# A mixture-of-experts layer on one core: the first token page gathered ahead of the sorting, the arrangement in the second pass, recurrence constants behind the modulation, the overflow branch behind the stores

## The chip, the cores and the metric

One core of a Trainium2 chip runs one hand-written kernel. The metric is the device time of the whole program in microseconds (us), the median over several runs; a profile is one further execution with the hardware profiler. The engines are TensorE (PE; its weight loads are shown apart as PEld), VectorE (DVE), ScalarE (ACT), GpSimd (POOL) and SyncE (SP, which issues nearly all DMA transfers here). Each engine works through its own queue in order and waits for others by semaphores.

## The reference

A layer with 256 latent tokens and 256 context tokens of width 1024: modulation, an input projection, a bidirectional recurrence (RG-LRU) beside a pooling group, an output projection, and then a top-4-of-32 mixture of experts, which has nearly all the weights. All is in float32. Cut to what matters:

```
mod_l = silu(c) @ w_mod + b_mod
h     = layer_norm(x + pos) * (1 + sc1) + sh1
z     = h @ w_in                                # 1536 columns
log_a = -8 * r * softplus(-lam)                 # recurrence constants
x1    = layer_norm(alpha * x + g1 * (mix @ w_out))
t     = x1 * (1 + sc2) + sh2                    # 256 tokens
logits = t @ router_w + router_b
top_v, top_i = top_k(logits, 4);  top_p = softmax(top_v)
for e in range(32):                             # only the chosen tokens count
    gu  = t @ w1[e] + b1[e]                     # w1[e]: 1024 x 2048
    act = clamped_swiglu(gu)
    out += gate[:, e] * (act @ w2[e] + b2[e])   # w2[e]: 1024 x 1024
y = layer_norm(alpha * x1 + g2 * out) * ln2_g + ln2_b
```

## The kernel before, in words

**Weights.** All weights come through a list made ahead of time, `plan` (L66 on): modulation weights, input projection, output projection, then for each expert position p the eight blocks of `w1` and the four blocks of `w2` of position p - 1. A block is 1024 KB. `due()` (L133) hands the next entries of the list to whichever slot of SBUF has come free, in the order in which slots come free, and `load()` issues them on SP. There are 12 ring slots, and eight more that earlier stages give up. The first two expert positions are always experts 0 and 1, so their weights need no index; from position 2 on, `source()` (L103) reads the expert's number from `ord_i` into a register of SP (L106).

**Prefix.** x and ctx are normalised and turned (`norm0`, `turn0`); the modulation vectors come from `gemv` and `mod_cols` (L370 to L380), and DVE and ACT apply shift and scale block by block (L437). In the program text the recurrence constants `hgb`, `aln` and the softplus of `lru_lambda` (L394 to L417, some 28 small DVE operations and an Exp on ACT) stand between the first modulation vector and the second. PE then makes the projections z (`z_block`, L444), followed by convolution, gates, scan, pooling, output projection, and the second norm.

**Routing.** `route`, `top4a`, `top4b` choose four experts for each token. `place(h)` (L677) counts, for each token and expert, how many earlier tokens chose it: `posm`, the token's place in the expert's list. For h = 1 it calls `sort` (L699): DVE compares the counts and makes the permutation S, two small matmuls (L710, L711) bring expert numbers and counts into that order, `ord_i` and `exc_i` are copied out. `softmax` (L791) makes the gates.

**Expert loop.** Chosen tokens are put into groups of 32 slots; expert position p has `SEQ[p]` groups (56 in all), and four groups make a page. For a page, `maps` (L816) builds a 0/1 matrix Pm from `slot` and a column of posm, `gather` (L836, two halves of 16 matmul passes, into the PSUM tile "misc") multiplies by it to bring the tokens into slots, and ACT copies the result to `xe`. `column` takes the first two positions' columns from posm and gate themselves, later ones from `placed`, which is in sorted order. `gated` (L826) makes Pg, Pm times the gates, and `turn_map` (L849) turns it, for `combine` (L926), which adds the results to the token accumulators acc[t][h].

A pass serves one or two groups of one expert: `gemm1` (L855) with eight k-steps, bias, `swiglu`, then `second` (L1036), which runs `gemm2` (L904) of the pass before. `gemm1` takes `hooks`: at k-step i it calls hooks[i], so other PE work is put between its steps: `turn` (turns the activations of the pass before, hook 1), `turn_map` (hook 3), `gather` of the next page (hooks 4 and 6). All these use the one PSUM tile "misc", emptied by ACT or DVE. `retire` gives slots of an expert's last pass back, one block at each k-step.

`arrange` (L942) stands before the first pass: posm and gate are turned (L948), brought into sorted order by S (L960, giving `placed`), and the experts' output biases, as Y, are added to acc with the gates (L968).

**Order.** The section from the expert loop on has a fixed order of instructions on each engine, the order of the program text.

**End.** Behind the last pass's `turn` comes `overflow()` (L977): all engines read the largest excess over a group's capacity into a register, and where it is positive they run a body that handles the surplus tokens. Then `second` of the last pass, `combine`, the last norm (`moments`, `scales`, `finish`) and the stores.

Of the kernel before, what the change touches and what calls it, by code (L numbers as in the profile page):

```python
# [56 lines left out]
def hybrid(tc, a, out):  # L57
# [175 lines left out]


# [4 lines left out]
    with ExitStack() as px:  # L239
# [171 lines left out]
        for n in (13, 11, 9, 7, 5, 3, 1):  # L411
# [5 lines left out]
        dve.tensor_scalar(hs, l0, -4.0, None, op0=ALU.mult)  # L417

        pool.iota(slot, pattern=[[1, P]], base=1, channel_multiplier=0, allow_small_or_imprecise_dtypes=True)
        tri = sb.tile([P, P], BF16, name="tri")  # L420
        one1 = sb.tile([P, 1], BF16, name="one1")
        ones = one1.to_broadcast([P, P])
        pool.memset(one1, 1.0)
        pool.memset(tri, 1.0)
        pool.affine_select(
            out=tri, in_=tri, pattern=[[1, P]], compare_op=ALU.is_gt, fill=0.0, base=0, channel_multiplier=-1
        )

        pool.tensor_scalar(x, x, ALPHA, None, op0=ALU.mult)
        sc1 = mod_cols(1, C_BM + 8, 1.0)  # L430
        for j in range(KD):
            for i in range(2):
                seg = hT(j)[:, T * i : T * i + T]
                if j % 2:
                    act.activation(seg, seg, AF.Identity, bias=sh1[:, i, j : j + 1], scale=sc1[:, i, j : j + 1])
                else:
                    dve.tensor_scalar(seg, seg, sc1[:, i, j : j + 1], sh1[:, i, j : j + 1], op0=ALU.mult, op1=ALU.add)  # L437

# [238 lines left out]
        def place(h):  # L677
# [18 lines left out]
            if h:  # L696
                sort(pp[:, 1, :], pp[:, 2, 0:1])

        def sort(cnt, cntc):  # L699

            key = sb.tile([P, NE], F32, name="key")
            keyc = sb.tile([P, 2], F32, name="keyc")
            dve.scalar_tensor_tensor(key, cnt, 64.0, col(C_KR, NE), op0=ALU.mult, op1=ALU.add)
            dve.scalar_tensor_tensor(keyc[:, 0:1], cntc, 64.0, col(C_KC), op0=ALU.mult, op1=ALU.add)
            dve.tensor_copy(keyc[:, 1:2], cntc)
            dve.tensor_scalar(key, key, keyc[:, 0:1], None, op0=ALU.is_gt)
            dve.tensor_reduce(keyc[:, 0:1], key, axis=AX.X, op=ALU.add)
            dve.tensor_scalar(S, col(C_RK, NE), keyc[:, 0:1], None, op0=ALU.is_equal)
            sp2 = mm.tile([1, 2, NE], F32, tag="mm", name="sp2")
            pe.matmul(sp2[:, 0, :], col(C_EI)[0:NE], S[0:NE], start=True, stop=True)  # L710
            pe.matmul(sp2[:, 1, :], keyc[0:NE, 1:2], S[0:NE], start=True, stop=True)  # L711
            for c in range(4):
                dve.tensor_scalar(SM[:, c, :], S, col(C_MASK + c), None, op0=ALU.mult)
            dve.tensor_copy(ord_i, sp2[:, 0, :])
            exc = key[0:1]
            dve.tensor_tensor(exc, sp2[:, 1, :], cols[0:1, C_CAP : C_CAP + NE], op=ALU.subtract)
            dve.tensor_scalar(exc, exc, 0.0, None, op0=ALU.max)
            dve.max(cmx, exc)
            dve.tensor_copy(exc_i[:, 0:NE], exc)
            dve.tensor_copy(exc_i[:, NE : NE + 1], cmx[:, 0:1])  # L720

# [29 lines left out]
        place(0)  # L751
        residual(1)
        top4a(1, lp)
        top4b(1)
        bp = mm.tile([P, T], F32, tag="mm", name="bp")
        for c in range(4):
            pe.matmul(
                bp[32 * c : 32 * c + 32, :],
                ident[:, 32 * c : 32 * c + 1].to_broadcast([P, 32]),
                bgrow[:, 1, :],  # L760
                start=True,
                stop=True,
                skip_group_check=True,
            )
        place(1)
        act.activation(g2s, bp, AF.Copy)
        donate("aa")
# [22 lines left out]

    def softmax(h):  # L791
        lh, nh = lg[:, h, :], ng[:, h : h + 1]
        dve.tensor_scalar(lh, lh, mx[:, h, 0:1], None, op0=ALU.subtract)
        act.activation(lh, lh, AF.Exp)
        dve.tensor_tensor(lh, lh, ge[:, h, :], op=ALU.mult)
        dve.tensor_reduce(nh, lh, axis=AX.X, op=ALU.add)
        dve.reciprocal(nh, nh)
        dve.tensor_scalar(gate[:, h, :], lh, nh, None, op0=ALU.mult)

# [35 lines left out]

    def gather(Pm, xe, k4):  # L836

        gx = misc([P, 4, P])
# [102 lines left out]

    def arrange():  # L942

        gt = misc([P, 4, P])
        for m, src in enumerate((posm, gate)):
            for h in range(2):
                for c in range(4):
# [7 lines left out]
                    )  # L955
        GT = spare[:, 0:4]
        act.activation(GT, gt, AF.Copy)
        so = misc([P, 4, NE])
        for m in range(4):
            pe.matmul(so[:, m], GT[0:NE, m], S[0:NE], start=True, stop=True)  # L960
        dve.tensor_copy(placed, so)
        for c in range(4):
            dve.scalar_tensor_tensor(
                Y[:, T * c : T * c + T], b2, col(C_MASK + c), g2s, op0=ALU.mult, op1=ALU.mult
            )
        for h in range(2):
            for t in range(2):
# [9 lines left out]
    def overflow():  # L977

        n_max = nc.values_load(exc_i[0:1, NE : NE + 1], engines=engines, min_val=0, max_val=T)
        with tc.If(n_max > 0, preferred_fallthrough_block=False):  # L980
# [11 lines left out]
            with tc.For_i(0, NE, 1) as i:  # L992
                n_i = nc.values_load(exc_i[0:1, bass.ds(i, 1)], engines=engines, min_val=0, max_val=T)
                with tc.If(n_i > 0):
# [15 lines left out]
                    for j in range(2):  # L1010
                        with tc.If(n_i > P * j):
# [41 lines left out]
    for n, (p, gs) in enumerate(passes):  # L1053
# [37 lines left out]
    turn(done[0], aT)  # L1091
    overflow()
    second(*done[1:], aT)
    back = (Y, PgT)

# [32 lines left out]

    for t in range(2):
        for h in range(2):  # L1130
            combine(*back, t, h, 0, 256)
            combine(*back, t, h, 256, 512)
            dve.bn_stats(st[:, t, h, :], acc[t][h])  # L1133
            if (t, h) == (1, 0):
                scales(0)
                finish_pool(0, 1)
        moments(t)
    finish(0, 0)
    store(0, 0)
    store(0, 1)  # L1140
    scales(1)
    finish_pool(1, 1, 256)
    finish(1, 0)
    store(1, 0)
    finish(1, 1, 0, 256)
    store(1, 1)
    order.close()
# [94 lines left out]
```

## Time and profile before

| | us |
|---|---|
| median of 3 runs | 1142.4 |
| the three runs | 1142.13, 1142.4, 1144.59 |
| the profiled execution's own time | 1143.31 |
| its span in the profile | 1141.6 |
| PE busy | 987.2 (86%) |
| DVE busy | 304.3 (27%) |
| ACT busy | 164.4 (14%) |
| POOL busy | 54.9 (5%) |
| bytes moved | 444.78 MB, 390 GB/s in the mean |

The span runs from the first to the last instruction of the profiled execution; its own time has 1.7 us more around it. A matmul that reads float32 is shown as two records. Of the 444.78 MB nearly all are weights, in blocks of 1024 KB. The granted clock of PE over the span is 0.945 of full speed.

### The profile page before, as it was taken

Reading aid. Unit: us, or ns where it says so; the run is one execution under the profiler, and the core shown is the slowest. Engines: PE = TensorE matmul, PEld = TensorE weight load, DVE = VectorE, ACT = ScalarE, POOL = GpSimd, SP = SyncE. Lnnn points to the kernel's source line nnn. Section 1 sums busy time; section 2 is a strip of 40 time slices with the busy share of each in tenths; the row PEclk is TensorE's granted clock in tenths of the full one; section 3 lists DMA queues with packets and bytes.
Section 4 is the critical chain, followed back from the end, with each engine's and each line's share of the span. In section 5 each row is a group of like instructions: output and inputs, shape, how many; then the busy total and the mean of one; then the engine's idle time right before and its main releaser. Section 6 shows DMA issues by size and latency. Waiting matters only on the chain. (4 is left out here: it accounts for less than half of the span.)

```text
span 1141.6 us, 21794 instructions
## 1 busy us (share of the span) xinstructions
PE 987.2 (86%) x9237; PEld 422.3 (37%) x9238; DVE 304.3 (27%) x803; ACT 164.4 (14%) x347; POOL 54.9 (5%) x73
## 2 busy tenths in 40 slices
PE   7799987999999968969997797869989887999663
PEld 3356554344334412424433232324433233443222
DVE  5436461132123121121321211212131221313104
ACT  3245331101110100101000110000100110110001
POOL 2128200000000000000000000000000000000001
PEclk9899998999999988979999999989999898999896
DMA  9999683999999999999999999999999999999992
GB/s 355 350 379 368 265 351 115 417 416 416 416 417 417 417 418 417 415 417 415 416 417 416 416 416 416 417 417 416 417 416 417 417 416 417 417 414 407 416 405 100
DMA packets 89862, 444.78 MB, mean 390 GB/s; under 512 B 9304, under 2 KB 15576, under 8 KB 56992
## 3 DMA queue, kind: packets, MB, share of 16 engines
q1 hardware_dynamic: 89528, 443.01, 96.0%
q8 instruction: 75, 1.23, 0.4%
q10 hardware_dynamic: 232, 0.32, 0.1%
q14 instruction: 27, 0.22, 0.1%
HBM read 442.25 MB, written 1.05 MB: 388 GB/s over the span
## 5 line engine op out<-in xcount | busy, mean ns | idle before, releaser
L862 PE MATMUL ph<-blk,xe 128*32 128x512 f32 x3584 | 427.8, 608 | 48.9 <-DMA blk<-in_w_dram 48.1
L911 PE MATMUL py<-blk,aT 128*32 128x256 f32 x3584 | 226.0, 405 | 67.1 <-DMA blk<-in_w_dram 60.5
L862 PEld LDWEIGHTS ph<-blk,xe 128*32 128x32 f32 x3584 | 103.7, 111 | 292.2 <-issue 170.5
L911 PEld LDWEIGHTS py<-blk,aT 128*32 128x32 f32 x3584 | 118.2, 116 | 185.5 <-issue 71.9
L924 DVE TENSOR_TENSOR Y<-py,g2s 32x256 f32<-32x256 f32 x224 | 94.2, 420 | 245.1 <-PE py L911 242.3
L889 DVE TENSOR_SCALAR av<-ph 128x256 f32<-128x256 f32 x56 | 23.6, 422 | 481.0 <-PE ph L876 481.0
L902 ACT ACTIVATE aT<-misc 128x256 f32<-128x256 f32 (+1 forms) x38 | 18.4, 485 | 395.1 <-PE misc L901 386.6
L845 ACT ACTIVATE xe<-misc,AB 128x128 f32<-128x128 f32 x112 | 42.1, 456 | 172.3 <-PE misc L842 172.3
L842 PEld LDWEIGHTS misc<-Pm,blk 128*128 128x128 f32 x448 | 54.0, 197 | 27.3 <-issue 22.6
L842 PE MATMUL misc<-Pm,blk 128*128 128x128 f32 x448 | 59.4, 288 | 4.3 <-DVE Pm L821 2.5
L444 PE MATMUL zp<-blk 128*128 128x256 f32 (+1 forms) x192 | 59.8, 468 | 3.7 <-DVE blk L437 3.7
L876 PE MATMUL ph<-b,SM 128*32 128x512 f32 x448 | 57.5, 616 | 0.0
L890 ACT ACTIVATE sgm<-av 128x256 f32<-128x256 f32 x56 | 23.3, 416 | 217.6 <-DVE av L889 217.6
L928 PE MATMUL acc<-Y,PgT 128*128 128x512 f32 (+1 forms) x120 | 51.9, 576 | 0.5 <-DVE Y L924 0.5
L1122 POOL TENSOR_TENSOR blk<-blk 128x512 f32<-128x512 f32 (+1 forms) x2 | 2.0, 992 | 977.0 <-ACT blk L1121 977.0
L444 PEld LDWEIGHTS zp<-blk 128*128 128x128 f32 x192 | 37.3, 196 | 25.7 <-issue 21.6
L928 PEld LDWEIGHTS acc<-Y,PgT 128*128 128x128 f32 x120 | 21.4, 189 | 31.2 <-issue 21.4
L876 PEld LDWEIGHTS ph<-b,SM 128*32 128x32 f32 x448 | 15.0, 114 | 35.6 <-issue 35.6
L590 PE MATMUL acc<-blk 128*128 128x512 f32 x64 | 27.8, 592 | 0.0
L892 DVE SCALAR_TENSOR_TENSOR av<-l,av 128x256 f32<-128x256 f32 x56 | 23.8, 425 | 10.9 <-ACT sgm L890 9.4
L359 PE MATMUL gp<-blk,csil 128*32 128x256 f32 x384 | 22.6, 382 | 2.4 <-DMA blk<-in_w_mod_dram 2.4
L893 DVE TENSOR_TENSOR av<-av,sgm 128x256 f32<-128x256 f32 x56 | 23.8, 425 | 1.9
(211 smaller groups left out, 451.3 us busy)
## 6 DMA issues: line engine op xcount, KB each, us to landing
blk<-in_w_dram SPq DMA_DIRECT2D x383, 1024.0 KB, 20.0
blk<-in_w_mod_dram SPq DMA_DIRECT2D x23, 1024.0 KB, 10.6
blk<-in_w_in_dram SPq DMA_DIRECT2D x6, 1024.0 KB, 16.9
blk<-in_w_out_dram SPq DMA_DIRECT2D x4, 1024.0 KB, 5.2
blk<-in_ctx_dram SPq DMA_DIRECT2D x2, 512.0 KB
blk<-in_x_dram SPq DMA_DIRECT2D x2, 512.0 KB
blk<-in_w_mod_dram SPq DMA_DIRECT2D x2, 512.0 KB, 16.4
blk<-in_w_dram SPq DMA_DIRECT2D x2, 512.0 KB
```

The source lines that it names most:

```text
L444: pe.matmul(zp[:, :n], w[:, k, P * half : P * half + P], hT(k)[:, :n], start=(k == 0), stop=(k == KD - 1))
L590: pe.matmul(acc[h][half], mixT[:, k, P * h : P * h + P], weight("out", k // 2)[:, k % 2, 512 * half : 512 * half + 512], start=(k == 4), s ...
L842: pe.matmul(gx[:, kk], xn[:, t, P * k : P * k + P], Pm[:, t], start=(t == 0), stop=(t == 1))
L845: act.activation(xe[:, k], gx[:, kk], AF.Identity, bias=AB[:, 1, k : k + 1], scale=AB[:, 0, k : k + 1])
L862: pe.matmul(ph[32 * c : 32 * c + 32], x[:, k], wv[:, :, c, :], start=(k == 0), stop=False, skip_group_check=True,)
L876: pe.matmul(ph[32 * c : 32 * c + 32], sel[c].to_broadcast([P, GS]), b1, start=False, stop=True, skip_group_check=True,)
L889: dve.tensor_scalar(av, ph[:, 0, :], 7.0, None, op0=ALU.min)
L892: dve.scalar_tensor_tensor(av, l1, 8.0, av, op0=ALU.min, op1=ALU.mult)
L893: dve.tensor_tensor(av, av, sgm, op=ALU.mult)
L911: pe.matmul(py[32 * c : 32 * c + 32, i], aT[:, i, k % 2, k // 2, :], W[k // 2][:, k % 2, T * c : T * c + T], start=(k == 0 and i == 0), st ...
L924: dve.tensor_tensor(dst[:, T * c : T * c + T], py[r, i], g2s[r], op=ALU.mult)
L928: pe.matmul(acc[t][h][:, lo:hi], PgT[:, P * t : P * t + P], Y[:, 512 * h + lo : 512 * h + hi], start=False, stop=False, skip_group_check=True,
```

## The change

Four things are done. The names are those above.

1. **First page ahead of the sorting.** `sort` is split. `place(1)` only makes `key` and `keyc`, which are now persistent tiles; then the maps of page 0 are built, and the comparisons of `sort_a` and the gates (`softmax_b`) follow. On PE the first gather half stands ahead of `sort_b`'s two matmuls, which use a "ph" tile; the second half goes into the tile "py". The subtraction and Exp of the softmax (`softmax_a`) move into the prefix.
2. **Arrangement in the second pass.** `arrange` is split into three. In pass 1, hook 0 is `arrange_a` (turning posm and gate), hook 1 `turn`, hook 2 `arrange_b` (sorted order, `placed`, the maps of page 1, the biases Y), hook 3 `turn_map`, hooks 4 and 6 the two gather halves of page 1, and `arrange_c` (biases to acc) stands before `second`. Pass 0 has no hooks. GT has a tile of its own. In later pages with two passes the second gather half moves from hook 4 to hook 5.
3. **Constants later.** The recurrence constants stand behind the loop that applies the modulation.
4. **Branch behind the stores.** `overflow`'s branch stands after the last norm and the stores; its register loads stand ahead of the last position's gemm1, and its body ends with a second `last_norm()` without the combine.

```
-            if h:
-                sort(pp[:, 1, :], pp[:, 2, 0:1])
+                dve.scalar_tensor_tensor(key, pp[:, 1, :], 64.0, col(C_KR, NE), op0=ALU.mult, op1=ALU.add)
+                dve.scalar_tensor_tensor(keyc[:, 0:1], pp[:, 2, 0:1], 64.0, col(C_KC), op0=ALU.mult, op1=ALU.add)
+                dve.tensor_copy(keyc[:, 1:2], pp[:, 2, 0:1])
...
+    def sort_a():
+        dve.tensor_scalar(key, key, keyc[:, 0:1], None, op0=ALU.is_gt)
+        dve.tensor_reduce(keyc[:, 0:1], key, axis=AX.X, op=ALU.add)
+        dve.tensor_scalar(S, col(C_RK, NE), keyc[:, 0:1], None, op0=ALU.is_equal)
...
+    def sort_b(sp2):
+        pe.matmul(sp2[:, 0, :], col(C_EI)[0:NE], S[0:NE], start=True, stop=True)
+        pe.matmul(sp2[:, 1, :], keyc[0:NE, 1:2], S[0:NE], start=True, stop=True)
+        dve.tensor_copy(ord_i, sp2[:, 0, :])
...
-    softmax(0)
-    softmax(1)
-    spare = wk.tile([P, KD, P], F32, name="xe")
+    GT = wk.tile([P, 4, P], F32, name="GT", bufs=1)
     ahead = page_maps(0)
-    for k4 in range(2):
-        gather(*ahead, k4)
+    sort_a()
+    for h in range(2):
+        softmax_b(h)
+    gather(*ahead, 0)
+    sort_b(ps.tile([1, 2, NE], F32, tag="ph", name="sp2", bufs=2))
     Pg = gated(0, ahead[0])
+    gather(*ahead, 1, "py")
     act.activation(wk.tile([P, 1], F32, name="sgm0", bufs=1), zero, AF.Sigmoid)
-    arrange()
...
-            hooks[3] = lambda PgT=PgT, Pg=Pg: turn_map(PgT, Pg)
-            if more:
+            if n:
+                hooks[3] = lambda PgT=PgT, Pg=Pg: turn_map(PgT, Pg)
+            if more and n:
                 ahead = page_maps(page + 1)
-        if more and len(of_page[page]) == 2:
-            hooks[4 if at else 6] = lambda at=at: gather(*ahead, at)
+        if n == 1:
+            hooks = {0: arrange_a, 2: arrange_b, 3: lambda: turn_map(PgT, Pg)}
+            hooks.update({4 + 2 * j: lambda j=j: gather(*ahead, j) for j in range(2)})
+        elif n and more and len(of_page[page]) == 2:
+            hooks[5 if at else 6] = lambda at=at: gather(*ahead, at)
...
+        if p == NE - 1:
+            n_max = nc.values_load(exc_i[0:1, NE : NE + 1], engines=engines, min_val=0, max_val=T)
...
+        if n == 1:
+            arrange_c()
         if done:
             second(*done[1:], aT)
...
     turn(done[0], aT)
-    overflow()
     second(*done[1:], aT)
...
+    last_norm((Y, PgT))
+    overflow()
```

PE from the last routing matmul (pp, L687 before and L701 after) to the first expert's gemm1 (ph); sp is the tile of the two sort matmuls, Pm the page map, Y the biases, blk weights or tokens. Before:

```order
L687 MATMUL pp<-one_337,selb 32x1
L710 MATMUL sp_1112<-S,cols 1x32
L711 MATMUL sp_1112<-S,keyc 1x32
L842 MATMUL misc<-Pm,blk 128x128 x16
L948 MATMUL misc<-ident,posm 32x128 x8
L948 MATMUL misc<-ident,gate 32x128 x8
L960 MATMUL misc<-S,xe 128x32 x4
L968 MATMUL acc<-Y,xe 128x512 x4
L862 MATMUL ph<-blk,xe 32x512 x32
```

After:

```order
L701 MATMUL pp<-one_306,selb 32x1
L847 MATMUL misc<-Pm,blk 128x128 x8
L793 MATMUL sp_1161<-S,cols 1x32
L794 MATMUL sp_1161<-S,keyc 1x32
L847 MATMUL py<-Pm,blk 128x128 x8
L867 MATMUL ph<-blk,xe 32x512 x64
L881 MATMUL ph<-b_72,SM 32x512 x8
```

The two sort matmuls now stand between the gather halves, the second of which writes to py; the matmuls of the arrangement have left this place. The first pass's gemm1 is in one piece.

PE in the second pass, from its first k-steps to the gemm2 (py from blk and aT); av are activations being turned, Pg the gated map. Before, from the last hooked work of the first pass on:

```order
L862 MATMUL ph<-blk,xe 32x512 x24
L842 MATMUL misc<-Pm,blk 128x128 x8
L862 MATMUL ph<-blk,xe 32x512 x8
L876 MATMUL ph<-b_72,SM 32x512 x8
L862 MATMUL ph<-blk,xe 32x512 x16
L901 MATMUL misc<-ident,av_1344 128x128 x2
L901 MATMUL misc<-ident,av_1345 128x128 x2
L862 MATMUL ph<-blk,xe 32x512 x24
L842 MATMUL misc<-Pm,blk 128x128 x8
L862 MATMUL ph<-blk,xe 32x512 x24
L876 MATMUL ph<-b_72,SM 32x512 x8
L911 MATMUL py<-blk,aT 32x256 x64
```

After:

```order
L953 MATMUL misc<-ident,posm 32x128 x8
L953 MATMUL misc<-ident,gate 32x128 x8
L867 MATMUL ph<-blk,xe 32x512 x8
L906 MATMUL misc<-ident,av_1287 128x128 x2
L906 MATMUL misc<-ident,av_1288 128x128 x2
L867 MATMUL ph<-blk,xe 32x512 x8
L967 MATMUL misc<-S,GT 128x32 x4
L867 MATMUL ph<-blk,xe 32x512 x8
L857 MATMUL misc<-ident,Pg 128x128 x2
L867 MATMUL ph<-blk,xe 32x512 x8
L847 MATMUL misc<-Pm,blk 128x128 x8
L867 MATMUL ph<-blk,xe 32x512 x16
```

The first two parts of the arrangement (posm, gate; S) now stand between gemm1's k-steps; the second gather half follows two k-steps later, and the third part (`acc<-Y,GT`) stands behind the bias and ahead of gemm2.

DVE in the prefix, from the last copy of the turned ctx (tr) to the modulation of the blocks (mc is the modulation's column, blk the tokens). Before, the end of that stretch (hgb and aln, L395 and L396, stand directly behind the copies):

```order
L412 TENSOR_TENSOR hs<-hs,l_307 128x8
L413 TENSOR_SCALAR hs<-hs 128x8
L414 SCALAR_TENSOR_TENSOR l_306<-l_306,hs 128x8
L415 TENSOR_SCALAR l_305<-l_305 128x8
L416 TENSOR_TENSOR l_305<-l_305,l_306 128x8
L417 TENSOR_SCALAR hs<-l_305 128x8
L380 SCALAR_TENSOR_TENSOR mc<-cp,cols 128x8 x2
L437 TENSOR_SCALAR blk<-blk,mc 128x256 x8
```

After:

```order
L337 COPY blk<-tr 128x2x256 x2
L394 SCALAR_TENSOR_TENSOR mc<-cp,cols 128x8 x2
L425 TENSOR_SCALAR blk<-blk,mc 128x256 x8
L429 TENSOR_SCALAR hgb<-cols 128x16
L430 TENSOR_SCALAR aln<-cols 128x16
L437 TENSOR_SCALAR l_375<-cols 128x8
L438 TENSOR_TENSOR l_376<-l_375,cols 128x8
```

The column mc and the modulation stand directly behind the copies, ahead of hgb and aln.

## Rows read from the trace of the kernel before

**Rows 1.** The page, achieved DMA rate in the 40 slices of 28.5 us.

```profile
GB/s 355 350 379 368 265 351 115 417 416 416 416 417 417 417 418 417 415 417 415 416 417 416 416 416 416 417 417 416 417 416 417 417 416 417 417 414 407 416 405 100
```

**Rows 2.** Stretches: bounds, length, busy us (instructions) per engine, clock, DMA share, GB/s.

```profile
172.00:175.20 3.20, 2.51 (x13) 2.54 (x14) 1.35 (x9) 0.00 (x0) 0.00 (x0) 0.67 1.03 407
175.20:195.40 20.20, 14.80 (x102) 8.21 (x104) 2.78 (x11) 4.98 (x11) 0.00 (x0) 0.80 0.04 8
...
200.00:1100.00 900.00, 793.79 (x8076) 313.36 (x8068) 196.66 (x550) 87.37 (x213) 0.00 (x0) 0.95 1.02 416
```

**Rows 3.** Timeline of PE, 168.6 to 192 us: start, length, instruction [idle before].

```profile
172.69 3.38 PE L842 MATMUL misc<-Pm,blk 128*128 128x128 f32 x16 [2.55 <-DVE Pm L821]
177.78 2.05 PE L842 MATMUL misc<-Pm,blk 128*128 128x128 f32 x16 [1.72 <-ACT xe L845]
181.43 0.65 PE L948 MATMUL misc<-ident,posm 128*32 128x128 f32 x16 [1.59 <-ACT xe L845]
...
183.43 1.91 PE L960 MATMUL misc<-S,xe 32*128 32x32 f32 x8 [0.92 <-ACT xe L957]
186.51 5.50 PE L968 MATMUL acc<-Y,xe 128*128 128x512 f32 x8 [1.17 <-DVE Y L963]
191.94 0.64 PE L862 MATMUL ph<-blk,xe 128*32 128x512 f32 x4
```

**Rows 4.** Timeline of DVE, the same stretch.

```profile
168.91 0.15 DVE L705 COPY keyc<-pp 128x1 f32<-128x1 f32 x1
...
171.97 0.74 DVE L821 TENSOR_SCALAR Pm<-slot,posm 128x64 f32<-128x64 f32 x4
```

**Rows 5.** Timeline of PE, 210 to 420 us.

```profile
229.49 7.09 PE L911 MATMUL py<-blk,aT 128*32 128x256 f32 x128
...
244.47 7.07 PE L862 MATMUL ph<-blk,xe 128*32 128x512 f32 x64
...
270.66 3.70 PE L928 MATMUL acc<-Y,PgT 128*128 128x512 f32 x8
```

**Rows 6.** Timeline of DVE, 26 to 38 us.

```profile
26.26 5.35 DVE L396 TENSOR_SCALAR aln<-cols 128x16 f32<-128x16 f32 x1
...
36.54 0.23 DVE L380 SCALAR_TENSOR_TENSOR mc<-cp,cols 128x8 f32<-128x8 f32 x2
```

**Rows 7.** Timeline of PE, 26 to 46 us.

```profile
33.24 0.61 PE L377 MATMUL cp<-ident,part 128*128 128x8 f32 x4 [0.50 <-ACT part L373]
37.57 8.70 PE L444 MATMUL zp<-blk 128*128 128x512 f32 x13 [3.72 <-DVE blk L437]
```

**Rows 8.** Timeline of all engines, 14 to 75 us.

```profile
16.12 10.85 SPq L156 DMA_DIRECT2D blk<-in_w_in_dram  x2
...
26.20 5.38 POOL L429 TENSOR_SCALAR blk<-blk 128x2048 f32<-128x2048 f32 x1 [20.14 <-PE tr L317]
```

**Rows 9.** The page's DMA issues: count, KB each, median us to landing.

```profile
blk<-in_w_in_dram SPq DMA_DIRECT2D x6, 1024.0 KB, 16.9
```

**Rows 10.** Stretches, columns as in rows 2.

```profile
36.00:44.00 8.00, 6.43 (x9) 2.74 (x10) 3.34 (x14) 4.04 (x8) 0.00 (x0) 0.57 1.11 282
```

**Rows 11.** Timeline of PE, 1104 us to the end.

```profile
1113.91 0.69 PE L901 MATMUL misc<-ident,av 128*128 128x128 f32 x2
1121.19 5.92 PE L911 MATMUL py<-blk,aT 128*32 128x256 f32 x64 [6.59 <-issue]
```

**Rows 12.** The line of the branch: count, ns min/median/max, first and last start.

```profile
L980 SPq COMPARE_BRANCH  x2: 38/48/57, 1107.8 to 1123.6; - x2
L980 PEldq COMPARE_BRANCH  x2: 95/3091/6087, 1112.8 to 1114.9; - x2
```

**Rows 13.** Waits of SP: us in total, times, longest.

```profile
SPq L980 <- SPq L980: 15.1, 1, 15.1
```

**Rows 14.** Stretches, columns as in rows 2, behind SP's jump.

```profile
1123.20:1126.20 3.00, 3.00 (x37) 1.61 (x33) 0.00 (x0) 0.00 (x0) 0.00 (x0) 0.63 0.03 8
```

More of the change, by code (lines that the diff above doesn't have):

```diff
@@ L204, in hybrid @@
     cmx = const.tile([1, 8], F32, name="cmx")
+    key = const.tile([P, NE], F32, name="key")
+    keyc = const.tile([P, 2], F32, name="keyc")
     lnrow = const.tile([P, 2, T], F32, name="lnrow")
@@ L232, in spread, with softmax_a, softmax_b @@
             act.activation(dst[:, 512 * c2 : 512 * c2 + 512], bp.rearrange("p c n -> p (c n)"), AF.Copy)
+    def softmax_a(h):
+        lh = lg[:, h, :]
+        dve.tensor_scalar(lh, lh, mx[:, h, 0:1], None, op0=ALU.subtract)
+        act.activation(lh, lh, AF.Exp)
+    def softmax_b(h):
+        lh, nh = lg[:, h, :], ng[:, h : h + 1]
+        dve.tensor_tensor(lh, lh, ge[:, h, :], op=ALU.mult)
+        dve.tensor_reduce(nh, lh, axis=AX.X, op=ALU.add)
+        dve.reciprocal(nh, nh)
+        dve.tensor_scalar(gate[:, h, :], lh, nh, None, op0=ALU.mult)
     accp = es.enter_context(tc.tile_pool(name="acc", bufs=1, space=PSUM))
@@ L391, in hybrid @@
         turn0(0)
+        pool.iota(slot, pattern=[[1, P]], base=1, channel_multiplier=0, allow_small_or_imprecise_dtypes=True)
+        tri = sb.tile([P, P], BF16, name="tri")
+        one1 = sb.tile([P, 1], BF16, name="one1")
+        ones = one1.to_broadcast([P, P])
+        pool.memset(one1, 1.0)
+        pool.memset(tri, 1.0)
+        pool.affine_select(
+            out=tri, in_=tri, pattern=[[1, P]], compare_op=ALU.is_gt, fill=0.0, base=0, channel_multiplier=-1
+        )
+        pool.tensor_scalar(x, x, ALPHA, None, op0=ALU.mult)
+        sc1 = mod_cols(1, C_BM + 8, 1.0)
+        for j in range(KD):
+            for i in range(2):
+                seg = hT(j)[:, T * i : T * i + T]
+                if j % 2:
+                    act.activation(seg, seg, AF.Identity, bias=sh1[:, i, j : j + 1], scale=sc1[:, i, j : j + 1])
+                else:
+                    dve.tensor_scalar(seg, seg, sc1[:, i, j : j + 1], sh1[:, i, j : j + 1], op0=ALU.mult, op1=ALU.add)
         hgb = sb.tile([P, 16], F32, name="hgb")
@@ L417, in hybrid @@
         dve.tensor_scalar(hs, l0, -4.0, None, op0=ALU.mult)
[L419 to L437, printed above, removed]
         def z_block(blk, half, n):
@@ L696, in place @@
             if h:
-                sort(pp[:, 1, :], pp[:, 2, 0:1])
[L699 to L720, printed above, removed]
+                dve.scalar_tensor_tensor(key, pp[:, 1, :], 64.0, col(C_KR, NE), op0=ALU.mult, op1=ALU.add)
+                dve.scalar_tensor_tensor(keyc[:, 0:1], pp[:, 2, 0:1], 64.0, col(C_KC), op0=ALU.mult, op1=ALU.add)
+                dve.tensor_copy(keyc[:, 1:2], pp[:, 2, 0:1])
         def residual(h):
@@ L752, in hybrid @@
         residual(1)
+        softmax_a(0)
         top4a(1, lp)
@@ L764, in hybrid @@
             )
+        act.activation(g2s, bp, AF.Copy)
+        softmax_a(1)
         place(1)
-        act.activation(g2s, bp, AF.Copy)
         donate("aa")
@@ L789, in misc @@
         return ps.tile(shape, F32, tag="misc", name="misc")
[L791 to L798, printed above, removed]
+    def sort_a():
[6 more added lines that the diff above has]
+        dve.tensor_copy(ord_i, sp2[:, 0, :])
+        exc = key[0:1]
+        dve.tensor_tensor(exc, sp2[:, 1, :], cols[0:1, C_CAP : C_CAP + NE], op=ALU.subtract)
+        dve.tensor_scalar(exc, exc, 0.0, None, op0=ALU.max)
+        dve.max(cmx, exc)
+        dve.tensor_copy(exc_i[:, 0:NE], exc)
+        dve.tensor_copy(exc_i[:, NE : NE + 1], cmx[:, 0:1])
+        for c in range(4):
+            dve.tensor_scalar(SM[:, c, :], S, col(C_MASK + c), None, op0=ALU.mult)
     def column(m, h, p):
@@ L834, in gated, with gather @@
         return Pg
-    def gather(Pm, xe, k4):
-        gx = misc([P, 4, P])
+    def gather(Pm, xe, k4, tag="misc"):
+        gx = ps.tile([P, 4, P], F32, tag=tag, name=tag)
         for kk in range(4):
@@ L940, in combine_all, with arrange_a @@
                 combine(Y, PgT, t, h)
-    def arrange():
+    def arrange_a():
         gt = misc([P, 4, P])
@@ L955, in arrange, with arrange_b @@
                     )
-        GT = spare[:, 0:4]
         act.activation(GT, gt, AF.Copy)
+    def arrange_b():
+        nonlocal ahead
         so = misc([P, 4, NE])
@@ L961, in arrange @@
         dve.tensor_copy(placed, so)
+        ahead = page_maps(1)
         for c in range(4):
@@ L965, in arrange, with arrange_c @@
             )
+    def arrange_c():
         for h in range(2):
@@ L1026, in overflow @@
                 dve.tensor_scalar(num, num, 1.0, None, op0=ALU.add)
+            last_norm()
     def page_maps(page):
@@ L1127, in store, with last_norm @@
         sp.dma_start(ov[:, t, s], y2[:, t, s])
[L1129 to L1146, printed above, removed]
+    def last_norm(back=None):
+        for t in range(2):
+            for h in range(2):
+                if back:
+                    combine(*back, t, h, 0, 256)
+                    combine(*back, t, h, 256, 512)
+                dve.bn_stats(st[:, t, h, :], acc[t][h])
+                if (t, h) == (1, 0):
+                    scales(0)
+                    finish_pool(0, 1)
+            moments(t)
+        finish(0, 0)
+        store(0, 0)
+        store(0, 1)
+        scales(1)
+        finish_pool(1, 1, 256)
+        finish(1, 0)
+        store(1, 0)
+        finish(1, 1, 0, 256)
+        store(1, 1)
+    last_norm((Y, PgT))
+    overflow()
     order.close()
```

2 lines of the change are left out of this document (removed).

## The prediction, made before the changed kernel ran

> **What bounds the kernel now.** I read the 40 slices first. From slice 8 to the last but one the weights arrive at 405 to 418 GB/s; in slice 7 the rate falls to 115 [rows 1]. So the long expert loop runs at the pace of the weight stream, and the reader is to see in it only that a stream started earlier ends earlier by as much. The finer windows show the hole: 407 GB/s up to 175.2, 8 GB/s from 175.2 to 195.4, and 416 in the loop behind it [rows 2]; some 20 us of streaming are missing. The timeline says why. All 20 weight slots are full, and the first comes free when the first expert's GEMM has used a block; that GEMM starts at 191.94 [rows 3], although the last selection result is there at 168.91 + 0.15 = 169.1 [rows 4]. Between lie softmax, sort, page map, two gather halves and the arrangement, one after the other. Two smaller places: the start of the projections [rows 6, 7] and the end, where TensorE (PE) stands from its transpose at 1113.91 to 1121.19 [rows 11].
>
> **Gather ahead of sort, arrangement in the second pass.** VectorE (DVE) now builds the page map right behind the counts: four operations, 0.74 us [rows 4], ready at 169.8. PE's first gather half follows. Its row of before took 3.38 us behind an idle gap, the second half 2.05 [rows 3]; with only about a microsecond of idle left I take 2.05 (range 2.05 to 3.38). The two sort matmuls, 32 columns each, are smaller than the first arrangement group of 0.65 us [rows 3]; I take 0.3 for the pair. The second half goes into a PSUM bank of its own, so it no longer waits for ScalarE (ACT) to empty the first, as its row of before does: 2.05 more. Sum 169.8 + 2.05 + 0.3 + 2.05 = 174.2, and the GEMM starts there instead of at 191.94: **17.7 us** earlier (15.1 with both halves at 3.38). ACT fills the first four blocks of the gathered page during the second half, and the GEMM asks for them one by one. The softmax sums, masks and gates that DVE still does afterwards lie beside the first pass's GEMM, two groups of 7.07 [rows 5]. The order of experts is copied out about 2 us later than before; SyncE (SP) waits for it with all later expert loads behind it, but the first of those needs a freed slot at about 176, so this wait is covered.
>
> The arrangement comes back inside the second pass. Its first part runs from 181.43 to the end of its matmuls at 182.5, 1.1 us of PE; the second took 1.91 and the third 5.50 [rows 3], both in a stretch of lowered clock. For the second I take half, 0.95; for the third, eight passes of 128x512, the combine's row of the same shape and count, 3.70 [rows 5]. Together 5.8 us more between the start of the first GEMM and that of the first second-layer GEMM, which before was 229.49 - 191.94 = 37.6 [rows 3, 5] and becomes 43.4.
>
> Does the stream feel that? The first block is freed a quarter of 7.07 us, 1.8, after the GEMM starts, and the stream was back at 195.4 [rows 2], 3.5 after the start, so 1.7 go from freeing to flowing. A block of 1024 KB [rows 9], 1.049 MB, takes 2.5 us at 416 GB/s. The 16 first-layer blocks of experts 0 and 1 feed it for 40.3 us, to start + 43.8. The 17th slot is a second-layer block, free at start + 43.4 + 1.8 and flowing 1.7 later, at 46.9: a new hole of about **3.1 us**. Before, the same sum gave 37.6 + 3.5 = 41.1, ahead of 43.8. Net at the front 17.7 - 3.1 = 14.6.
>
> **Constants later.** DVE's queue holds the softplus chain ahead of the modulation. Its second operation stretches to 5.35 us beside the 5.38 us in which GpSimd (POOL) scales x [rows 6, 8], and the chain ends just before 36.54, where the modulation's scale is made [rows 6]; the product it waits for was done at 33.24 + 0.61 = 33.85, and PE starts 1.03 us after the scale, at 37.57 [rows 6, 7]. Behind the change the scale follows at 33.9 and PE at 34.9. The weights for it were issued at 16.12 [rows 8] and such blocks take 16.9 us in the median [rows 9], 33.0, so they hardly hold it up: **2.6 us**. The chain then runs beside the first projections; its consumer, the first gate exponential, comes three projections later. There is a second gain: behind PE's idle stretch the granted clock is 0.57 on average from 36 to 44, with PE busy 6.43 us of it [rows 10], so 6.43 x 0.43 = 2.8 us are lost to the clock there. With the gap down to 1 us this may be won or not: I take 2.0 of 0 to 2.8. From there to the selection PE is nearly always busy, so its start moves everything: 4.6 us.
>
> **Branch behind the stores.** Before, PE reaches the branch, and its jump alone takes 6087 ns from 1114.9 [rows 12], to 1121.0. Without it PE could start the last GEMM at about 1115.1. But SP waits at that branch for 15.1 us [rows 13] before its jump, last seen at 1123.6 [rows 12]; I read this wait as that for the last weights, landed at 1123.0, since the stream too has ended by then [rows 14]. The last of eight GEMM steps needs them, 5.92/8 = 0.7 us [rows 11]. The GEMM ends at 1123.8 instead of 1121.19 + 5.92 = 1127.1: 3.3 gained, not 6. At the end every engine now jumps after its last work. PE's 6.1 us lie beside normalisation and stores. SP ends last; its steps there cost 1123.6 - 1123.0 = 0.6. Its jump is bounded by its own 57 ns and by PE's 6.1 [rows 12]; 8 GB/s x 3 us = 24 KB were moved in the 3 us behind SP's jump, with no weight or store under way [rows 14], so I take half of that stretch, 1.5. Net 3.3 - 0.6 - 1.5 = **1.2 us**. The counts' register loads, now ahead of the last expert's GEMM, fall where PE waits for weights, and on SP behind the last weight issue: nothing.
>
> On that jump the Trainium skill (Runtime: NRT & Kernel Launch, Instruction fetch mechanics) says that a taken branch whose target lies outside the fetched window waits for a fetch; PE's row agrees, and by it the stall would not go away but move to whichever engine ends the program. That is the third rival below.
>
> **Sum.** 14.6 + 4.6 + 1.2 = 20.4 us. The profiled execution took 1143.3 us, 0.9 over the median of 1142.4; against its own time the sum gives 1122.9, against the median 1122.0. I predict **1122 us**; the bounds of the clock, the gathers and the jump put this case at 1117 to 1126.
>
> **Rivals.**
> - *Second pass serialised* (0.12). Six steps of that pass share one PSUM bank, and five times the next one waits for ACT or DVE to empty it; the GEMM's steps between them are meant to cover that. At the front such a round left PE idle 1.72 us, and again 1.59 [rows 3]. If all five were exposed, the hole grows by 8.5: 1130.5. Against it: two groups' GEMM step is 1.8 long.
> - *No landing limit at the end* (0.08). If the last weights come as early as the loop's pace says, the full 6.1 is won without a price: 1117.
> - *The jump is paid after the stores* (0.14). The last engine jumps as PE did, 6.1 instead of 1.5: 1126.6.
> - *The constants were not on the path* (0.05). If the first projection weights hold PE until 37.6, the prefix gives nothing and that part of the change does not do what it says: 1126.6.
> - *Slower* (0.04). The one mechanism that reaches the other side is again the shared bank, with DVE as the late one: its queue holds the previous pass's activations and the next page's maps ahead of a bank's copy, and slots go unfreed. The price is five rounds; beyond 4.1 us each (20.4/5) more than is won and it is slower than before, over 1142.4; no row of before shows a round above 2.
>
> **Numbers.** The forecast has 0.57. The range 1114 to 1131 reaches 3 us below its bounds, for the second rival with a full clock gain, and above them over the first, third and fourth. A difference of 0.2%, 2.3 us, is about what a measurement of this kernel tells from none; all cases but the last are faster by more, and of the last 0.01 is within it: faster 0.96, same 0.01, slower 0.03.
>
> **What would show it.** Right: the first expert GEMM near 169.6 (174.2 less 4.6); the hole before it under 4 us; a dip of about 3 us some 44 us later; PE's first projection at about 35; the last GEMM starting without a gap, ending with the last weights; some 2 us more between the last store's landing and the end. Wrong: a first GEMM after 178, a weight stream that dips again later in the loop, or an end more than 5 us behind the stores.

## The result and the profile after

The changed kernel takes **1104.83 us** in the median of four runs (1103.31 to 1105.46), against 1143.27 us before in four: a ratio of 0.966, interval 0.9645 to 0.9678. That is 38.4 us, where the prediction had 20.4. 1104.8 lies below the range that was given.

The page of the profile after: PE's busy time, the DMA rate in 40 slices (now of 27.6 us), and the queue that carries the weights (packets, MB, share of the time of 16 engines).

```profile
PE 980.9 (89%) x9237; PEld 420.1 (38%) x9238; DVE 300.2 (27%) x803; ACT 164.6 (15%) x347; POOL 54.9 (5%) x73
...
GB/s 366 355 404 374 260 348 379 376 422 424 422 424 423 423 424 424 424 425 424 423 424 424 424 423 424 423 425 423 424 422 425 425 423 424 425 423 414 424 422 135
...
q1 hardware_dynamic: 89528, 443.01, 97.4%
```

The dip to 115 of [rows 1] is gone; the seventh and eighth slices have 379 and 376. But the loop now stands at 422 to 425 where it had 414 to 418, and even the first slice, which lies ahead of nearly everything that the change moves, has 366 instead of 355.

Stretches of the kernel after (bounds, length, busy us and instructions per engine, granted clock, DMA share, GB/s):

```profile
8.00:16.00 8.00, 6.21 (x9) 1.46 (x8) 6.06 (x17) 5.64 (x7) 0.00 (x0) 1.00 1.03 421
33.00:44.00 11.00, 9.92 (x20) 4.64 (x20) 7.12 (x37) 5.53 (x10) 0.00 (x0) 0.72 0.94 300
170.00:175.00 5.00, 5.00 (x47) 1.60 (x50) 0.49 (x4) 2.99 (x6) 0.00 (x0) 1.00 0.64 233
175.00:180.00 5.00, 5.00 (x52) 1.56 (x48) 0.00 (x0) 0.00 (x0) 0.00 (x0) 1.00 0.98 369
210.00:215.00 5.00, 5.00 (x40) 2.27 (x40) 3.34 (x13) 0.65 (x2) 0.00 (x0) 1.00 0.85 360
215.00:220.00 5.00, 5.00 (x100) 3.03 (x96) 0.00 (x0) 0.00 (x0) 0.00 (x0) 1.00 0.67 234
300.00:1000.00 700.00, 621.40 (x6310) 246.04 (x6306) 155.61 (x440) 67.30 (x165) 0.00 (x0) 0.95 1.02 423
```

The hole of 20 us at 8 GB/s [rows 2] has shrunk to 5 x (1 - 233/423) + 5 x (1 - 369/423) = 2.9 us. A new dip at 210 to 220 is 5 x (1 - 360/423) + 5 x (1 - 234/423) = 3.0 us. And from 8 to 16 us, where both kernels do the same work in the same order, the rate is 421; before:

```profile
8.00:16.00 8.00, 6.14 (x8) 1.26 (x7) 5.83 (x17) 5.67 (x7) 0.00 (x0) 1.00 1.03 409
```

PE's timeline after, first the start of the projections, then from the first gather half on:

```profile
34.59 23.11 PE L458 MATMUL zp<-blk 128*128 128x512 f32 x48 [1.08 <-DVE blk L425]
```

```profile
166.12 2.02 PE L847 MATMUL misc<-Pm,blk 128*128 128x128 f32 x16 [1.12 <-DVE Pm L826]
...
168.28 2.05 PE L847 MATMUL py<-Pm,blk 128*128 128x128 f32 x16
170.26 13.94 PE L867 MATMUL ph<-blk,xe 128*32 128x512 f32 x128
...
187.81 1.07 PE L867 MATMUL ph<-blk,xe 128*32 128x512 f32 x8 [0.68 <-DVE l L896]
...
210.02 3.70 PE L978 MATMUL acc<-Y,GT 128*128 128x512 f32 x8
213.65 7.11 PE L916 MATMUL py<-blk,aT 128*32 128x256 f32 x128
```

The projections start at 34.59 instead of 37.57 [rows 7]; both gather halves are of the short kind, 2.02 and 2.05, without the waits of [rows 3]; the first expert GEMM starts at 170.26 instead of 191.94, 21.7 us earlier. The biases to acc (L978) take 3.70 ahead of the first second-layer GEMM, 213.65 - 170.26 = 43.4 us behind the first GEMM.

The end, PE's timeline and the line of the branch:

```profile
1079.47 0.69 PE L906 MATMUL misc<-ident,av 128*128 128x128 f32 x2
1081.46 6.73 PE L916 MATMUL py<-blk,aT 128*32 128x256 f32 x64 [1.30 <-DVE Y L929]
1088.73 3.79 PE L933 MATMUL acc<-Y,PgT 128*128 128x256 f32 x16 [0.54 <-DVE Y L929]
```

```profile
L989 PEldq COMPARE_BRANCH  x2: 91/1708/3325, 1090.1 to 1092.9; - x2
...
L989 SPq COMPARE_BRANCH  x2: 38/48/57, 1100.0 to 1102.0; - x2
```

The 6.59 us in front of the last GEMM [rows 11] are down to 1.30, where the prediction had no gap. PE's jump now takes 3325 ns and lies beside the last norm; SP's is as short as before, and the span ends 1.8 us behind its start at 1102.0.

### The profile page after: what moved, and what is told of

Read it like the earlier page. It is cut to its first block, busy times and chain, and to the rows that moved or that the text cites. A ratio compares the mean times of both kernels' runs of the same rounds, so it can differ in the third digit from the quotient of the medians.

```text
span 1103.8 us, 21803 instructions
## 1 busy us (share of the span) xinstructions
PE 980.9 (89%) x9237; PEld 420.1 (38%) x9238; DVE 300.2 (27%) x803; ACT 164.6 (15%) x347; POOL 54.9 (5%) x73
## 3 DMA queue, kind: packets, MB, share of 16 engines
q1 hardware_dynamic: 89528, 443.01, 97.4%
## 4 chain that ended last, share of the span: by engine, by line
PE 55%; DMA 42%; DVE 2%; ACT 0%; issue 0%; ACTq 0%; SPq 0%; DVEq 0%
DMA blk<-in_w_dram 40%; PE ph L867 22%; PE py L916 12%; PE zp L458 5%; PE misc L847 3%; DMA blk<-in_w_mod_dram 2%; PE acc L604 2%; PE acc L933 2%; PE ph L881 2%; PE gp L373 1%; PE acc L488 1%; PE misc L906 1%; PE bp L233 1%; DMA cols<-in_cols_dram 0%; PE misc L857 0%; PE acc L718 0%
## 5 line engine op out<-in xcount | busy, mean ns | idle before, releaser
L916 PE MATMUL py<-blk,aT 128*32 128x256 f32 x3584 | 221.8, 400 | 54.5 <-DMA blk<-in_w_dram 49.8
L847 PEld LDWEIGHTS misc<-Pm,blk 128*128 128x128 f32 x432 | 51.4, 195 | 23.8 <-issue 23.8
L847 PE MATMUL misc<-Pm,blk 128*128 128x128 f32 x432 | 56.5, 285 | 1.1 <-DVE Pm L826 1.1
L906 PEld LDWEIGHTS misc<-ident,av 128*128 128x128 f32 x112 | 11.9, 144 | 32.9 <-issue 32.1
## 6 DMA issues: line engine op xcount, KB each, us to landing
blk<-in_w_mod_dram SPq DMA_DIRECT2D x2, 512.0 KB, 16.2
```

The costliest lines, as they stand in the source:

```text
L916: pe.matmul(py[32 * c : 32 * c + 32, i], aT[:, i, k % 2, k // 2, :], W[k // 2][:, k % 2, T * c : T * c + T], start=(k == 0 and i == 0), st ...
```

## The experiments

**The place of the weight slots.** The changed kernel makes `key` and `keyc` persistent, 160 bytes of each partition ahead of the weight slots. In the built programs the first slot starts at byte 29024 before and at 29184 after; the others follow in steps of 8192 bytes, so all share the remainder. Five kernels leave n bytes unused there and change nothing else (in the changed kernel the line stands behind `keyc`):

```
     cmx = const.tile([1, 8], F32, name="cmx")
+    const.tile([P, n // 4], F32, name="gap")     # n = 160, 32, 96 before; 32, 256 after the change
     lnrow = const.tile([P, 2, T], F32, name="lnrow")
```

> The kernel before, with 160 bytes per partition left unused ahead of the weight slots, so that the first slot starts at byte 29184 (a multiple of 512) as in the changed kernel, instead of 29024 (a multiple of 32 alone). Theory A, the slots' place in SBUF sets the rate of the weight stream: loop at 423 GB/s instead of 416, about 390 MB at that difference, so 15 to 18 us off, 1125 to 1128 us. Rival B, the order of the work sets the rate (fewer or other waits of SP): still 416 GB/s and 1143 us.

Measured 1127.68 us against 1144.04 before, ratio 0.987 (0.9849 to 0.9895). The kernel before with 160 bytes unused, in the stretches 8 to 16 and 300 to 1000 us:

```profile
8.00:16.00 8.00, 6.25 (x9) 1.51 (x8) 6.12 (x17) 5.59 (x7) 0.00 (x0) 1.00 1.02 419
300.00:1000.00 700.00, 617.76 (x6266) 243.23 (x6262) 150.44 (x422) 68.68 (x169) 0.00 (x0) 0.96 1.02 424
```

> The kernel before with 32 bytes unused ahead of the slots: first slot at 29056, a multiple of 64 and 128 but not of 256. Theory A with a step of 64 or 128 bytes: 423 GB/s and 1125 to 1128 us as with 160 bytes; A with a step of 256 or 512 bytes: still 416 and 1143. Rival B: 1143.

Measured 1143.86 us, ratio 1.000 (0.999 to 1.0011). Its loop:

```profile
300.00:1000.00 700.00, 605.14 (x6154) 237.86 (x6150) 150.46 (x422) 66.58 (x164) 0.00 (x0) 0.95 1.02 416
```

> The kernel before with 96 bytes unused ahead of the slots: first slot at 29120, a multiple of 64 but not of 128. Theory A with a step of 64 bytes: 423 GB/s and 1125 to 1128 us; with a step of 128 or more: 1143. Rival B: 1143.

Measured 1144.66 us, ratio 1.0005 (0.9996 to 1.0015). Its loop:

```profile
300.00:1000.00 700.00, 606.53 (x6150) 237.44 (x6146) 149.85 (x421) 66.64 (x165) 0.00 (x0) 0.95 1.02 416
```

> The changed kernel with 32 bytes unused ahead of the slots: first slot at 29216, a multiple of 32 alone, as before the change. Theory A: the loop falls back to 416 GB/s, 15 to 18 us more, 1120 to 1123 us, which is what the prediction's own sum gave. Rival B: 423 GB/s and 1105 us.

Measured 1125.25 us, ratio 0.984 (0.9825 to 0.9858). Its loop:

```profile
300.00:1000.00 700.00, 610.91 (x6156) 239.54 (x6148) 149.46 (x420) 66.36 (x163) 0.00 (x0) 0.94 1.02 415
```

> The changed kernel with 256 bytes unused ahead of the slots: first slot at 29440, a multiple of 256 but not of 512. If the rate of the stream needs a multiple of 256, loop at 423 GB/s and 1105 us; if it needs 512, loop at 416 and 1121 to 1125 us. Rival, that the move itself matters and not the multiple: something in between.

Measured 1106.33 us (1105.79 to 1106.55). Its loop:

```profile
300.00:1000.00 700.00, 617.37 (x6294) 243.92 (x6290) 154.97 (x438) 67.69 (x166) 0.00 (x0) 0.96 1.02 423
```

This settles theory A. The order of the work is the same in each pair, and the rate follows the address: 423 to 424 GB/s with the first slot at 29184 and 29440, remainder 0 on division by 256; 415 to 416 at 29024, 29056, 29120 and 29216, remainders 96, 128, 192 and 32. A multiple of 128 is not enough, a multiple of 512 is not needed. All tiles behind the unused bytes move with the slots; that the slots are what counts rests on the rate differing from 8 us on and on nearly all bytes going there (443.01 of 444.8 MB are on the weights' queue). Why the multiple matters is not shown.

It is worth 1144.04 - 1127.68 = 16.4 us on the kernel before, and on the changed one 1125.25 less 1104.83 or 1106.33, 18.9 to 20.4 us; 1125.25 lies 2 us above what was expected. PE's timeline of the changed kernel with 32 bytes unused, the start of the projections and the first expert GEMM:

```profile
35.52 23.51 PE L459 MATMUL zp<-blk 128*128 128x512 f32 x48 [1.33 <-DMA blk<-in_w_in_dram]
171.59 13.94 PE L868 MATMUL ph<-blk,xe 128*32 128x512 f32 x128
```

Here the slower stream also holds up the prefix: the projections wait for their weights until 35.52 (34.59 in the changed kernel, where they wait for DVE), and the first expert GEMM starts at 171.59 instead of 170.26.

The remaining kernels undo one part of the change each, with the slots at 29184.

**Constants back.** The block of constants stands ahead of the modulation again.

```
         turn0(0)
+        hgb = sb.tile([P, 16], F32, name="hgb")
...
+        dve.tensor_scalar(hs, l0, -4.0, None, op0=ALU.mult)
         pool.iota(slot, pattern=[[1, P]], base=1, channel_multiplier=0, allow_small_or_imprecise_dtypes=True)
```

> The changed kernel with the recurrence constants back ahead of the modulation (slots stay at 29184). The prediction's step: projections start 2.6 to 3.0 us later and 2.0 us of lowered clock come back, so 1109.4 (4.6 more). Rival, the weights of the first projection or later work hide it: 1105 to 1106.

Measured 1109.35 us (1108.69 to 1109.68), 4.5 more. PE's timeline, and the stretch 33 to 44 us:

```profile
32.55 0.61 PE L391 MATMUL cp<-ident,part 128*128 128x8 f32 x4 [0.50 <-ACT part L387]
37.57 8.78 PE L457 MATMUL zp<-blk 128*128 128x512 f32 x13 [4.40 <-DVE blk L450]
```

```profile
33.00:44.00 11.00, 6.60 (x10) 2.79 (x10) 5.82 (x29) 4.04 (x8) 0.00 (x0) 0.53 0.98 309
```

The product for the scale is there at 33.2, but the projections start at 37.57, 3.0 later than after the change, and the granted clock of the stretch is 0.53 instead of 0.72. The first expert GEMM starts at 173.94, 3.7 later, so 0.7 of it are the clock's in this pair of profiles. A second profile of the changed kernel (1106.25 us) has another split:

```profile
34.02 22.25 PE L458 MATMUL zp<-blk 128*128 128x512 f32 x48 [1.08 <-DVE blk L425]
168.83 13.94 PE L867 MATMUL ph<-blk,xe 128*32 128x512 f32 x128
```

Against it the projections start 3.55 later and the first GEMM 5.1, so 1.6 are the clock's.

**Arrangement first.** All three parts stand ahead of the first pass again, in the new gather order.

```
+    arrange_a()
+    arrange_b()
+    arrange_c()
     lngb, PgT, done = None, None, None
...
-            hooks = {0: arrange_a, 2: arrange_b, 3: lambda: turn_map(PgT, Pg)}
+            hooks = {3: lambda: turn_map(PgT, Pg)}
```

> The changed kernel with all three parts of the arrangement back ahead of the first pass, its gather order and all else kept. The prediction's step: the first GEMM starts later by the arrangement's own chain, 8 to 12 us, the dip of about 3 us some 44 us later goes away, so 1110 to 1114. Rival, the hole is filled later anyway: within 1 us of 1104.8.

Measured 1112.83 us (1112.06 to 1113.43), 8.0 more. PE's timeline from the arrangement to the first expert GEMM:

```profile
170.28 0.64 PE L953 MATMUL misc<-ident,posm 128*32 128x128 f32 x16
...
173.94 1.07 PE L966 MATMUL misc<-S,GT 32*128 32x32 f32 x8 [2.57 <-ACT GT L961]
176.18 5.40 PE L976 MATMUL acc<-Y,GT 128*128 128x512 f32 x8 [1.17 <-DVE Y L969]
181.51 13.94 PE L867 MATMUL ph<-blk,xe 128*32 128x512 f32 x128
```

The first GEMM starts 11.3 us later, the dip of 3.0 us is gone (421 to 429 GB/s from 210 to 230), and 11.3 - 3.0 = 8.3.

**Sort first.** The sort and the softmax sums stand ahead of the page map, and both gather halves share one PSUM tile.

```
-    ahead = page_maps(0)
     sort_a()
+    sort_b(ps.tile([1, 2, NE], F32, tag="ph", name="sp2", bufs=2))
     for h in range(2):
         softmax_b(h)
+    ahead = page_maps(0)
     gather(*ahead, 0)
-    sort_b(ps.tile([1, 2, NE], F32, tag="ph", name="sp2", bufs=2))
     Pg = gated(0, ahead[0])
-    gather(*ahead, 1, "py")
+    gather(*ahead, 1)
```

> The changed kernel with the sort, its two matmuls and the softmax sums back ahead of the page map, and both gather halves in the one PSUM tile; the arrangement stays in the second pass. The prediction's step: first gather 2.4 us later, second half 1.7 us later, and up to 1.3 us of lowered clock: 1109 to 1110.5. Rival, the first GEMM is bound by ACT filling the gathered page: within 1 us of 1104.8.

Measured 1115.36 us (1114.26 to 1116.53), 10.5 more, about twice what was expected. PE's timeline and two stretches (the clock is the last but two):

```profile
170.38 3.75 PE L847 MATMUL misc<-Pm,blk 128*128 128x128 f32 x16 [3.77 <-DVE Pm L826]
175.86 3.78 PE L847 MATMUL misc<-Pm,blk 128*128 128x128 f32 x16 [1.72 <-ACT xe L850]
179.57 14.02 PE L867 MATMUL ph<-blk,xe 128*32 128x512 f32 x128
```

```profile
170.00:175.00 5.00, 3.75 (x16) 3.49 (x16) 1.04 (x7) 0.70 (x3) 0.00 (x0) 0.50 0.34 137
175.00:180.00 5.00, 4.14 (x20) 3.69 (x24) 0.00 (x0) 1.12 (x4) 0.00 (x0) 0.52 0.00 0
```

The first half waits 4.3 us longer for the map (170.38 against 166.12, with DVE's whole sorting ahead of it), the second waits 1.72 for ACT, and behind the idle gap of 3.77 us the clock is at 0.50 to 0.52, its lower level of 1.2 GHz, so the halves take 3.75 and 3.78 instead of 2.02 and 2.05: 4.3 + 1.7 + 3.5 = 9.5, and the GEMM starts 179.57 - 170.26 = 9.3 later. The expectation had the gap too short and lowered clock for less than one half.

**Branch back.** The branch and its register loads stand ahead of the last GEMM again.

```
     turn(done[0], aT)
+    overflow()
     second(*done[1:], aT)
...
     last_norm((Y, PgT))
-    overflow()
```

> The changed kernel with the branch and its register loads back ahead of the last GEMM. The prediction's step, with the last weights as the limit: 1.2 us more, 1106; by the two traces' last stretches (last weights to end 18.6 and about 16.3 us) 2.3 more, 1107. Rival, no landing limit: up to 6.1 more, 1111. Rival, the jump costs the same behind the stores: 1105.

Measured 1108.50 us (1107.82 to 1109.88), 3.7 more, between the expected 1.2 to 2.3 and the 6.1 of the rival. PE's timeline at the end:

```profile
1079.11 0.69 PE L906 MATMUL misc<-ident,av 128*128 128x128 f32 x2
1086.10 2.78 PE L916 MATMUL py<-blk,aT 128*32 128x256 f32 x22 [6.30 <-issue]
1089.07 3.25 PE L916 MATMUL py<-blk,aT 128*32 128x256 f32 x42 [0.19 <-issue]
```

PE stands for 6.30 us again, and the last GEMM ends at 1089.07 + 3.25 = 1092.32, 13.2 us after its transpose started; without the branch 1088.19, 8.7 after: 4.5 gained. From the GEMM's end to the end of the span it is 1106.8 - 1092.32 = 14.5 with the branch ahead and 1103.8 - 1088.19 = 15.6 with it behind: 1.1 paid. The last weights, in the kernel before, in this kernel and in the changed one (the last figure is GB/s):

```profile
1122.50:1123.00 0.50, 0.50 (x12) 0.30 (x8) 0.00 (x0) 0.00 (x0) 0.00 (x0) 0.50 0.00 0
```

```profile
1086.50:1087.00 0.50, 0.50 (x12) 0.30 (x8) 0.00 (x0) 0.00 (x0) 0.00 (x0) 0.50 0.19 57
1087.00:1087.50 0.50, 0.50 (x12) 0.30 (x8) 0.00 (x0) 0.00 (x0) 0.00 (x0) 0.50 0.00 0
```

```profile
1087.00:1087.50 0.50, 0.50 (x12) 0.01 (x2) 0.00 (x0) 0.00 (x0) 0.00 (x0) 0.94 0.02 8
```

No transfer of them starts after 1122.5 in the kernel before, and none after about 1087 in the other two. The changed kernel's last GEMM ends about 1 us behind them, which fits the limit that the prediction set; with the branch ahead it ends over 5 us behind them.

**Biases later.** A variant that might beat the change: the third part of the arrangement stands behind the second-layer matmuls of its pass, ahead of DVE's copy of their result to Y.

```
-        if n == 1:
-            arrange_c()
         if done:
-            second(*done[1:], aT)
+            second(*done[1:], aT, arrange_c if n == 1 else None)
```

> The changed kernel with the third part of the arrangement (output biases, 3.70 us of PE) behind the second-layer matmuls of the second pass instead of ahead of them, so that second-layer slots come free 3.7 us earlier. If the dip of about 3 us in the weight stream at 210 to 220 us is late freeing of these slots, it goes away: 1102 us. Rival, the stream makes the dip up later or another wait takes its place: 1104.8.

Measured 1103.38 us (1102.28 to 1103.94). Its stretches where the changed kernel has its dip:

```profile
210.00:215.00 5.00, 5.00 (x100) 2.99 (x93) 2.46 (x11) 0.42 (x1) 0.00 (x0) 1.00 1.00 424
215.00:220.00 5.00, 5.00 (x35) 1.96 (x28) 1.27 (x4) 0.00 (x0) 0.00 (x0) 1.00 1.02 428
220.00:225.00 5.00, 5.00 (x52) 1.60 (x48) 2.56 (x7) 0.60 (x1) 0.00 (x0) 1.00 0.97 393
225.00:230.00 5.00, 5.00 (x50) 1.44 (x46) 0.00 (x0) 0.39 (x1) 0.00 (x0) 1.00 1.00 383
```

The rate holds through 220; 0.8 us are missing behind it. A second comparison, both kernels on one chip:

> The changed kernel unaltered, beside the variant with the biases later on the same chip: 1103.5 to 1105.5 us by both theories.

Measured 1105.16 us (1104.58 to 1106.25).

> The variant with the third part of the arrangement behind the second-layer matmuls, beside the changed kernel on the same chip. The dip of 3.0 us in the weight stream had shrunk to about 0.8 in its profile, so 2 us less than the changed kernel, 1102 to 1103.5. Rival, the 1.4 us of the first comparison were chance: no difference.

Measured 1103.93 us (1103.79 to 1104.54), all five runs below the changed kernel's five. Its stretches in this comparison:

```profile
210.00:215.00 5.00, 5.00 (x100) 3.03 (x96) 3.28 (x12) 0.45 (x2) 0.00 (x0) 1.00 0.99 392
215.00:220.00 5.00, 5.00 (x44) 2.23 (x34) 0.83 (x2) 0.00 (x0) 0.00 (x0) 1.00 0.99 362
```

With 413 and 381 GB/s in the next two stretches, 1.7 us are missing from 210 to 230 by the sum used above, against 3.2 in the changed kernel's profile beside it (239, 341, 433 and 409 GB/s): the dip shrank by 1.5 us, in the first comparison by 2.4 (3.2 to 0.8). The variant is the fastest kernel of this study, by 1.2 to 1.5 us, a tenth of a per cent and below what the prediction took as measurable from few runs. Half to three quarters of the dip are thus the late freeing of second-layer slots; that the rest is too is not shown, and why not all of the shrinking arrives at the end was not followed up.

## Why the prediction was wrong

The mechanisms were right and their sum nearly so; one term of the time was not in the sum at all.

- **The step that failed** is the first one: "the reader is to see in it only that a stream started earlier ends earlier by as much". It takes the rate of 416 GB/s as given. The change raised it to 423, which over the 374 MB of 900 us is 900 x (1 - 416/423) = 15 us, 16.4 as measured by itself. No mechanism for it was among the rivals. The diff had it in plain sight: two tiles became persistent, and they stand ahead of the slots in SBUF. The Trainium skill (DMA: Bandwidth & Descriptors, How a descriptor splits into AXI transactions) says that the first transaction of a descriptor that does not start at a multiple of 256 bytes begins at the multiple below, and that the bytes before the start are fetched, not used, and still cost. The page speaks of reading; here it is the side written to, in SBUF, that was moved. The runs agree with the multiple. They do not show a cost that grows with the bytes wasted: remainders 32 and 192 give 415 and 416.
- **Without it**, with the slots off the multiple again (remainder 32, before 96), the change takes 1125.25 against 1144.04: 18.8 us (16.2 to 20.0 by the interval), where the sum was 20.4 and the bounds of its case 1117 to 1126. That it comes so near is in part luck, since misses of both signs meet in it. The branch gave more than its term, while the first expert GEMM starts 191.94 - 171.59 = 20.35 us earlier there, for 17.7 + 4.6 = 22.3: the prediction had the weights of the projections landed at 33.0 and hardly in the way, and in that kernel PE waits for them until 35.52, which leaves 37.57 - 35.52 = 2.1 us for 2.6.
- **Front**, predicted 14.6: the first GEMM starts 21.7 us earlier, 3.7 of that from the constants, so 18.0 for 17.7; the dip is 3.0 for 3.1, at the place given; 15.0 together. Undone one at a time the two parts cost 8.0 and 10.5, 3.5 more than together. The lowered clock explains part of that: undone alone, the sort brings 3.5 us of it in the halves and the arrangement 1.7 in the biases (5.40 for 3.70), 5.2 in sum, against an estimated 4.0 for both in [rows 3] (3.38, 1.91 and 5.50 less the 2.02, 1.07 and 3.70 of the changed kernel). The rest was not followed up.
- **Constants**, predicted 4.6: 4.5. The split was otherwise, 3.0 to 3.55 from the start instead of 2.6, and 0.7 to 1.6 from the clock to the first GEMM instead of 2.0, so the total is right by luck; the projections' start had been put at 34.9 and was 34.59.
- **Branch**, predicted 1.2: 3.7. The sum charged 2.1 us behind the stores, 1.5 of it for SP's jump as a guess between 0.06 and 6.1; 1.1 were paid. And the GEMM's end came 4.5 earlier instead of 3.3. The prediction took the last weights as landed at 1123.0, from SP's wait, but no weights start to move there from 1122.5 on, some 0.5 us earlier; the other 0.7 were not followed up. The rival that the jump is paid in full at the end did not come: PE's 3.3 us lie beside the norm, and the jump of SP, which ends last, took at most 57 ns.
- **Rivals**: the second pass was not serialised. PE's one idle time among the six steps on the shared bank is 0.68 us, ahead of 187.81, and it ends with DVE's activations of the first pass, not with the bank.
- **Together**, the place of the slots first: 16.4 us, and from there 1127.68 - 1104.83 = 22.9 for the rest, whose terms add up to 15.0 + 4.5 + 3.7 = 23.2; each comes from runs that scatter by about 1 us. The two make 39.2, against 38.4 in the first comparison, where the kernel before stood at 1143.27. In the other order the rest gives 18.8 and the place 20.4, so the two are not independent. Of the 4 us between the orders the traces show 1.3 at the first expert GEMM (171.59 against 170.26) and about 2 in the loop, where the changed kernel off the multiple has 415 GB/s and the kernel before 416.

## What to carry to other kernels

When a stream of transfers bounds a kernel, its rate is a term of the sum like any other: before costing what is moved, ask whether the edit shifts the tiles that the stream writes to, and compare the rate of an early stretch that the edit doesn't touch. A new small tile in a pool ahead of large ones is enough, and here it was worth 16 us; keep the destinations at multiples of 256 bytes. And work that one removes from in front of a full set of slots may be put where it delays the next freeing; the price can be worked out from the number of slots, as it was here.

## What the runs showed of the hardware

The rate of 1 MB weight transfers on one queue was 423 to 424 GB/s with destinations at multiples of 256 bytes and 415 to 416 GB/s at the four other remainders tried, some 1.8% apart, while the DMA engines showed the same busy share of 1.02 in both. The reason is not shown, and no run shows a loss that grows with the remainder. A gather of 16 passes took 3.75 us behind a PE gap of 3.77 us, at a granted clock of 0.50 (1.2 GHz), and 2.02 behind a gap of 1.12 us, at 1.00 (2.4 GHz).
